# A hybrid decoder trunk on one core: branch gates by seven products, the residual stream in DRAM, h in whole rows

## The chip, the core and the metric

The kernel runs on one core of a Trainium2 chip. The core has a matrix engine (TensorE, PE in the profile; its weight loads are PEld), a vector engine (VectorE, DVE), a scalar engine (ScalarE, ACT), GpSimd (POOL), which here only issues accumulating DMAs, and SyncE (SP), which issues nearly all other DMAs. Each engine works through its own queue in order and waits on semaphores. Matmul results land in PSUM, where the kernel holds eight tiles (banks) of 128 x 512 floats; everything else on chip lives in SBUF. The metric is the device time of one execution in microseconds (us); the median of the runs is given, and one further execution was profiled.

## What is computed

Two decoder layers over one sequence of 512 positions with 1024 channels, float32. In each layer three sub-layers add to a residual stream x:

```python
h = rms_norm(x, gn[0])
x = x + 0.5 * rms_norm(swiglu(h, w_ffn1_gate[l], w_ffn1_up[l], w_ffn1_down[l]), gn[1])
h = rms_norm(x, gn[2])
proj = h @ w_in[l]
hq, hf, hi, hg, aq, ak, av, gate_a, gate_b = jnp.split(proj, IN_SPLITS, axis=-1)
y_hg = hgrn2_mixer(hq, hf, hi, hg, lb_all[l], hgrn_head_gain[l]) @ w_branch_hgrn[l]
y_at = swa_sink_attention(aq, ak, av, attn_sinks[l]) @ w_branch_attn[l]
mixed = jax.nn.sigmoid(gate_a) * y_hg + jax.nn.sigmoid(gate_b) * y_at
x = x + rms_norm(mixed @ w_out[l], gn[3])
h = rms_norm(x, gn[4])
x = x + 0.5 * rms_norm(swiglu(h, w_ffn2_gate[l], w_ffn2_up[l], w_ffn2_down[l]), gn[5])
```

`swiglu` is `(silu(h @ w_gate) * (h @ w_up)) @ w_down` with 2816 inner channels. The mixer's projection has 4864 columns: four groups of 512 for a gated linear recurrence with four heads, attention queries (512), keys and values (128 each), and two groups of 1024 that gate the two branches (gate_a, gate_b).

## The kernel before

**Matmuls.** Every float32 operand of a large matmul is split into a rounded part (hi) and the rest (lo), and a product is three matmuls: hi x hi, hi x lo, lo x hi (`mm3`; line 103 issues each of them, line 110 the transposes). Weights are the stationary operand, 128 x 128 blocks; the moving operand is a row of h, 128 channels by 512 positions, or half of it (256). Only in `down` is it the other way round.

**Weights.** `Stream` brings them in units of 128 x 1024, eight blocks each. A unit is loaded by SyncE into one of four raw buffers (lines 184 and 187), and `split` makes hi on ScalarE (line 219) and lo. An item of kind u gets its lo from a subtraction on VectorE (line 226); kinds v, a and d get it from a negated copy on ScalarE (line 223) and an accumulating DMA from GpSimd (line 224). Items are split up to three ahead of the one in use (`AHEAD`), with six in flight at most.

**A pair of output blocks** (gate and up of an FFN, 128 columns each) can be computed in three ways. `project` runs through the eight blocks of one output with 512 positions a time. `twice` does the same in two halves of 256 positions. `fast` takes the pair as a 2 x 2 block matrix product (rows: the two outputs; columns: the two halves of the positions; the sum over 1024 channels in two halves of 512) and computes it by seven products of four blocks each instead of eight. For this it needs sums of weight quarters (items b and c: lines 206, 207, 212 and 213 on VectorE, in tiles `tt`), sums of the quarters of h (`sums()`, one call for two of the eight rows of h: line 496 adds hi and lo again, lines 344 to 347 make the combinations, lines 294 and 295 split them), and a recombination of the seven results on VectorE (lines 682, 684, 689, 690) and ScalarE (line 670).

**An FFN.** `quad` does the first two pairs. Then two pairs run by `twice` (`PLAIN` = 4 plain pairs; the very first FFN has `FIRST` = 6, in part by `project`), and the other 18 by `fast`. `gated` (lines 706, 707) applies the SiLU gate. `down` multiplies by the down weights with eight outputs at a time in all eight PSUM banks. Its last `TAIL` = 2 groups are done one block of 128 positions after the other: `post` scales the block (line 566) and adds it to the residual stream x (line 570), which stays in SBUF as `x_all` (16 KB in each partition), `norm` normalises it for the next sub-layer (lines 509 to 513, 576), and `turn` transposes it on TensorE and writes h as hi and lo. `Pre` holds h as whole rows (the mixer), `Halves` in one tile per row and half of the positions (the FFNs).

**The mixer.** `quad` projects heads 0 and 1 of the recurrence, then follow keys, queries and values, two token-wise projections, heads 2 and 3, and 16 branch steps: `branch` projects one block of 128 gate columns by `project`, takes tanh (line 1020), multiplies the branch output by four more blocks and joins both (line 1025). First the eight of the attention branch, then the eight of the recurrence branch. The recurrences of the heads and the attention blocks are generators that issue their small matmuls in between.

**Order.** TensorE's instructions keep the order in which the program writes them. That order is set by `Order`: a running estimate of TensorE's time, and for each generator a delay (`WAIT`) after which its next step is issued between two matmuls. The other engines' instructions are put in order by a planner when the kernel is built: program order is the priority, but ready work may go ahead of work that waits. Working tiles of 2 KB in a partition come from one pool (`big()`, 53 buffers, `SLOTS`); PSUM's eight banks are five `acc` and three `aux`.

## Time and profile before

| | us |
|---|---|
| median of the runs | 2177.47 |
| lowest run | 2176.96 |
| profiled execution | 2179.35 |
| its span in the profile | 2177.6 |
| TensorE busy (matmuls) | 2161.6 |
| VectorE busy | 1369.7 |
| ScalarE busy | 1043.5 |
| GpSimd busy | 124.2 |

The execution moves 262.55 MB by DMA, 121 GB/s on average. Times in the profile's views are microseconds from the start of the span unless marked ns. "Busy" for TensorE includes modelled pipeline ends, so two neighbouring matmuls overlap in it, and 99% busy does not say at what rate it works. A line number is a line of the kernel; a helper's line (103, 110, 219, 226) stands for everything that calls it, and the tile names behind it tell which.

### The profile page before, as it was taken

The page shows a single profiled execution, that of the slowest core. Times are in us where ns is not written, and L with a number is a line of the kernel's source. Part 1 is how long each engine was busy: PE and PEld are TensorE (multiplying, and loading weights), DVE is VectorE, ACT ScalarE, POOL GpSimd, SP SyncE. Part 2 cuts the span into 40 slices and gives each one's busy share as a digit, 9 for nine tenths or more (in the row PEclk, how much of TensorE's full clock was granted, in tenths as well). Part 3 has the DMA queues.
Part 4 walks back from the last instruction along what each step waited for, and adds up shares of the span by engine and source line. Part 5 has one row for each costly group of instructions (what it writes and reads, how often), then busy time and mean ns, then how long its engine had stood idle before and what let it go on. Part 6 is the DMA issues. An engine that isn't in the chain of part 4 may idle for free.

```text
span 2177.6 us, 34576 instructions
## 1 busy us (share of the span) xinstructions
PE 2161.6 (99%) x13625; PEld 1951.4 (90%) x13625; DVE 1369.7 (63%) x2381; ACT 1043.5 (48%) x1703; POOL 124.2 (6%) x148
## 2 busy tenths in 40 slices
PE   9999999999999999999999999999999999999998
PEld 7999988888888999998899998898788889999987
DVE  6887725856734768783487786267566438687823
ACT  6565515354423555562355554254543336565612
POOL 0111000000000011100001110000000000111000
PEclk9999999999999999999999999999999999999999
DMA  7587632211223258773237874322112332578721
GB/s 236 121 185 180 173 97 78 87 59 59 70 95 97 81 130 182 180 203 97 73 107 162 192 184 147 96 86 68 53 64 78 97 97 88 137 179 184 187 89 39
DMA packets 126131, 262.55 MB, mean 121 GB/s; under 512 B 13360, under 2 KB 71184, under 8 KB 125968
## 3 DMA queue, kind: packets, MB, share of 16 engines
q1 hardware_dynamic: 105088, 203.13, 29.7%
q0 software_dynamic: 20736, 57.16, 15.0%
q8 instruction: 107, 1.75, 0.3%
q14 instruction: 56, 0.46, 0.1%
q10 hardware_dynamic: 144, 0.05, 0.0%
HBM read 200.99 MB, written 2.15 MB: 93 GB/s over the span
## 4 chain that ended last, share of the span: by engine, by line
PE 95%; DVE 2%; DMA 1%; ACT 1%; issue 1%; SPq 0%; POOL 0%; DVEq 0%; POOLq 0%; ACTq 0%
PE acc L103 70%; PE aux L103 23%; PE aux L110 1%; DMA w<-wall 1%; PE acc L110 1%; DMA s<-xin 0%; DVE s L453 0%; DMA wlo<-w 0%; DVE s L940 0%; DVE wlo L226 0%; DVE s L771 0%; DMA g_sb<-gains 0%; DVE s L566 0%; ACT s L509 0%; DVE s L576 0%
## 5 line engine op out<-in xcount | busy, mean ns | idle before, releaser
L103 PE MATMUL acc<-s,whi 128*128 128x256 f32 (+1 forms) x5104 | 1096.1, 312 | 1.6 <-ACT whi L219 0.9
L103 PEld LDWEIGHTS acc<-s,whi 128*128 128x128 f32 x5104 | 833.2, 191 | 48.3 <-DVE s L701 1.1
L103 PE MATMUL acc<-s,wlo 128*128 128x256 f32 (+1 forms) x2552 | 791.0, 310 | 0.1
L219 ACT CAST whi<-w 128x1024 fp32r<-128x1024 f32 (+1 forms) x373 | 360.7, 969 | 664.0 <-PE aux L103 270.0
L226 DVE TENSOR_TENSOR wlo<-w,whi 128x1024 fp32r<-128x1024 f32 (+1 forms) x229 | 278.5, 1218 | 405.1 <-ACT whi L219 399.6
L103 PEld LDWEIGHTS acc<-s,wlo 128*128 128x128 f32 x2552 | 487.2, 191 | 26.2 <-DVE wlo L226 0.4
L103 PE MATMUL acc<-whi,s 128*128 128x512 f32 x1296 | 425.2, 393 | 0.0
L103 PEld LDWEIGHTS acc<-whi,s 128*128 128x128 f32 x1296 | 243.9, 188 | 51.3
L103 PE MATMUL acc<-wlo,s 128*128 128x512 f32 x648 | 252.9, 390 | 0.0
L224 POOL DMA_DIRECT2D wlo<-w x144 | 124.0, 861 | 1909.9 <-DVE s L347 689.0
L103 PE MATMUL aux<-whi,s 128*128 128x512 f32 x624 | 207.8, 390 | 0.0
L103 PE MATMUL aux<-s,whi 128*128 128x256 f32 x1120 | 204.6, 283 | 0.0
L226 DVE TENSOR_TENSOR wlo<-tt,whi 128x1024 fp32r<-128x1024 f32 x140 | 170.6, 1218 | 10.1 <-ACT whi L219 9.7
L103 PEld LDWEIGHTS aux<-s,whi 128*128 128x128 f32 x1120 | 174.7, 192 | 0.0
L219 ACT CAST whi<-tt 128x1024 fp32r<-128x1024 f32 x140 | 145.7, 1041 | 26.8 <-PE acc L103 26.3
L103 PE MATMUL aux<-s,wlo 128*128 128x256 f32 x560 | 158.5, 283 | 0.0
L103 PEld LDWEIGHTS acc<-wlo,s 128*128 128x128 f32 x648 | 122.1, 188 | 23.7
L103 PEld LDWEIGHTS aux<-whi,s 128*128 128x128 f32 x624 | 117.1, 188 | 24.1
L206 DVE TENSOR_TENSOR tt<-w,w 128x512 f32<-128x512 f32 x70 | 48.4, 691 | 126.8 <-DMA w<-wall 116.9
L223 ACT ACTIVATE wlo<-w 128x1024 fp32r<-128x1024 f32 (+1 forms) x144 | 122.0, 847 | 0.0
L103 PE MATMUL aux<-wlo,s 128*128 128x512 f32 x312 | 121.4, 389 | 0.0
L103 PEld LDWEIGHTS aux<-s,wlo 128*128 128x128 f32 x560 | 107.5, 192 | 0.0
(164 smaller groups left out, 1888.2 us busy)
## 6 DMA issues: line engine op xcount, KB each, us to landing
w<-wall SPq DMA_DIRECT2D x283, 512.0 KB, 3.5
w<-wall SPq DMA_DIRECT2D x352, 128.0 KB, 2.6
wlo<-w POOLq DMA_DIRECT2D x74, 512.0 KB, 6.0
wlo<-w POOLq DMA_DIRECT2D x70, 256.0 KB, 4.1
grow<-rows_d SPq DMA_DIRECT2D x6, 512.0 KB, 4.9
s<-xin SPq DMA_DIRECT2D x8, 256.0 KB, 6.7
y<-s SPq DMA_DIRECT2D x8, 256.0 KB, 2.5
w<-wall SPq DMA_DIRECT2D x2, 256.0 KB, 4.1
```

The lines of the kernel that those rows point to most:

```text
L103: nc.tensor.matmul(o, lhsT, rhs, start=start, stop=stop)
L110: nc.tensor.transpose(o, src, ident)
L206: nc.vector.tensor_tensor(self.t13[:, h[0]], w[:, h[0]], v[:, h[0]], op=ALU.add)
L219: i = nc.scalar.copy(it.hi[:, c], w[:, c])
L223: nc.scalar.mul(it.lo[:, c], w[:, c], -1.0)
L224: nc.gpsimd.dma_start(it.lo[:, c].bitcast(F32), w[:, c], accum_op=ALU.add)
L226: nc.vector.tensor_tensor(it.lo[:, c], w[:, c], it.hi[:, c].bitcast(F32), op=ALU.subtract)
```

## The change

- **Branch gates.** The 16 gate blocks of a mixer are taken in eight pairs by the seven products. The body of `fast` up to the recombination becomes `sevenths`, and `branches` uses it. Its results for the second block come out negated, which the sign of tanh's scale takes back. Since the weights lie in DRAM as before, `gates` builds two of the three units of a pair from two half-row loads each. Four `sums()` calls are made in the mixer, ahead of heads 2 and 3.
- **Residual stream.** `x_all` goes. x lives in a DRAM tile `x_d`; `down` loads its eight pieces (128 x 512) into working buffers one group ahead of its tail, and `post` stores each piece after the addition. The first layout of x goes to DRAM as well.
- **Working buffers.** `SLOTS` goes from 53 to 61, the room of `x_all`.
- **h.** `Halves`, `of_half` and `twice` go; all sub-layers hold h in whole rows, and `Pre` gets `sums` and `raw`. `sums` adds hi and lo in whole rows of 512.
- **FFN.** `PLAIN` is 3: after `quad`'s two pairs one pair is done by `project`, and 19 by `fast`. All four `sums()` calls now stand ahead of that one pair.

```diff
--- before.py
+++ after.py
@@ -27,14 +27,14 @@
-SLOTS = 53
+SLOTS = 61
...
-W32, WS, AHEAD, TAIL, PLAIN, FIRST, EARLY = 4, 6, 3, 2, 4, 6, 4
+W32, WS, AHEAD, TAIL, PLAIN, FIRST, EARLY = 4, 6, 3, 2, 3, 6, 4
 HEADS = (0, 4, 1, 5, 2, 6, 3, 7)
@@ -111,12 +111,11 @@
         order.t += 107.0
-    x_all = const([P, TT, D], "x_all")
-    xt = [[x_all[:, t, h * S : (h + 1) * S] for h in range(2)] for t in range(TT)]
     g_sb = const([P, DEPTH, 6, KT], "g_sb")
     nc.scalar.dma_start(g_sb, gains)
     xs = [big() for _ in range(KT)]
     nc.sync.dma_start(xs[0], xin[:, 0, :])
+    x_d = dr.tile([TT, 2, P, S], F32, name="x_d")
     rows_d = dr.tile([DEPTH * 6 * KT, P], F32, name="rows_d")
     ones = const([P, P], "ones")
     nc.vector.memset(ones, 1.0)
@@ -158,6 +157,15 @@
             for _ in range(n):
                 self.items += [Item("a", self.n), Item("b", self.n), Item("c", self.n), Item("d", self.n, 4)]
                 self.n += 2
+
+        def gates(self):
+
+            u, h = self.n, (slice(0, D // 2), slice(D // 2, D))
+            self.src[u + 1] = [(h[0], wall[u + 1][:, h[1]]), (h[1], wall[u + 2][:, h[0]])]
+            self.src[u + 2] = [(h[0], wall[u + 1][:, h[0]]), (h[1], wall[u + 2][:, h[1]])]
+            self.pairs(1)
+            self.plain(1)
         def rows(self, kt):
@@ -355,7 +363,7 @@
         def operand(self, n):
             if n in (1, 2, 4):
-                return [[v[:, i, :] for i in range(2)] for v in self.raw(n // 4, n > 1)]
+                return self.raw(n // 4, n > 1)
             x, i = (self.x56, n - 5) if n in (5, 6) else (self.x37, (n - 3) // 4)
             return [[v[:, i, :] for v in x[k]] for k in range(4)]
@@ -398,7 +406,9 @@
                     p = aux()
                     for k in range(4):
                         transpose(p[:, k * P : (k + 1) * P], xs[4 * h + k][:, t * P : (t + 1) * P])
-                    (nc.vector.tensor_copy if h else nc.scalar.copy)(xt[t][h], p)
+                    x = big()
+                    (nc.vector.tensor_copy if h else nc.scalar.copy)(x, p)
+                    nc.sync.dma_start(x_d[t, h], x)
                     yield WAIT["laid"]
             self.laid = True
@@ -419,9 +429,9 @@
                 x.append(v)
         def raw(self, half, i):
-            return [x[half + i] for x in self.x124]
-
-    class Pre:
+            return [[x[half + i][:, j, :] for j in range(2)] for x in self.x124]
+
+    class Pre(Quarters):
         def __init__(self, l, n):
@@ -430,6 +440,20 @@
             self.have = [0, 0]
             self.rb = None
             self.xn = {}
+            self.x56, self.x37 = [], []
+
+        def sums(self):
+            k = len(self.x56)
+            a = []
+            for hi, lo in (self.h[k], self.h[k + 4]):
+                f = big()
+                nc.vector.tensor_tensor(f, hi.bitcast(F32), lo.bitcast(F32), op=ALU.add)
+                a.append([f[:, c] for c in HALF])
+            for x, v in zip((self.x56, self.x37), quarter_sums(a[0][0], a[1][0], a[0][1], a[1][1])):
+                x.append(v)
+
+        def raw(self, half, i):
+            return [cut(self.h[k + 4 * i], HALF[half]) for k in range(4)]
         def turn(self, half, get):
@@ -456,50 +480,6 @@
                     )
                 self.have[half] += 2
-    class Halves(Pre, Quarters):
...
-        def sums(self):
-            k = len(self.x56)
-            f = [big(F32, [P, 2, S // 2]) for _ in range(2)]
-            for half in range(2):
-                for i in range(2):
-                    h = self.h[k + 4 * i][half].bitcast(F32)
-                    nc.vector.tensor_tensor(f[half][:, i, :], h[:, 0, :], h[:, 1, :], op=ALU.add)
-            for x, v in zip((self.x56, self.x37), quarter_sums(f[0][:, 0, :], f[0][:, 1, :], f[1][:, 0, :], f[1][:, 1, :])):
-                x.append(v)
-
-        def raw(self, half, i):
-            return [self.h[k + 4 * i][half] for k in range(4)]
-
     def rms(parts, n, between=lambda h: None):
         ss = small([P, 2], "ss2", 8)
@@ -521,7 +501,7 @@
         nc.sync.dma_start(grow, rows_d[(l * 6 + n) * KT : (l * 6 + n + 1) * KT, :].rearrange("k p -> (k p)").partition_broadcast(P))
         y = [[acc(), acc()], [acc(), acc()], [acc(), aux()], [aux(), aux()]]
-        pre = (Pre if nxt[1] == 2 else Halves)(*nxt) if nxt else None
+        pre = Pre(*nxt) if nxt else None
         def ready(n):
@@ -534,7 +514,13 @@
             mv = [w.rearrange("p (m two c) -> p m two c", two=2, c=P)[:, :, i, :] for w in b[2:]]
             mm3(y[t][h], st, mv, 2 * j + i == 0, 2 * j + i == kt - 1)
+        xt = [[None] * 2 for _ in range(TT)]
         for j in range(kt // 2 - TAIL):
+            if j == kt // 2 - TAIL - 1:
+                for t in range(TT):
+                    for h in range(2):
+                        xt[t][h] = big()
+                        nc.sync.dma_start(xt[t][h], x_d[t, h])
             for h in range(2):
                 ready(2 * j + 2 + EARLY)
                 b = ws.next(8, TT)
@@ -568,6 +554,8 @@
             rc = rms(y[t], D, scale)
             for h in range(2):
                 nc.vector.scalar_tensor_tensor(xt[t][h], yg[h], rc, xt[t][h], op0=ALU.mult, op1=ALU.add)
+                if pre:
+                    nc.sync.dma_start(x_d[t, h], xt[t][h])
         def norm(t):
             rc = rms(xt[t], D)
@@ -602,12 +590,6 @@
             order.until(lambda: left[0] == 0)
         return pre
-    def of_half(pre, k, half):
...
     def quad(pre, halves):
         o = [acc() for _ in range(4)]
@@ -620,17 +602,8 @@
                 for j in range(4):
                     if (k, j) not in blocks:
                         blocks[k, j] = ws.next(uses=2 if halves else 1)
-                    wmm(o[j][:, c], blocks[k, j], of_half(pre, k, half), k == 0, k == KT - 1)
+                    wmm(o[j][:, c], blocks[k, j], cut(pre.h[k], c), k == 0, k == KT - 1)
             ws.pinned = False
-        return o
-
-    def twice(pre):
-
-        o = acc()
-        blocks = [ws.next(uses=2) for _ in range(KT)]
-        for half in (0, 1):
-            for k in range(KT):
-                wmm(o[:, HALF[half]], blocks[k], of_half(pre, k, half), k == 0, k == KT - 1)
         return o
     def project(pre):
@@ -650,44 +623,52 @@
                 order.poll()
         return o
+    H2 = S // 2
+
+    def sevenths(pre, between=lambda: None):
+
+
+        def product(o, it, c, n):
+            x = pre.operand(n)
+            for k in range(4):
+                wmm(o, ws.block(it, c + k), x[k], k == 0, k == 3)
+
+        p1, p26, p57, p43 = acc()[:, :H2], acc(), acc(), aux()
+        s, v = big()[:, :H2], big(F32, [P, 2, H2])
+        m = sb.tile([P, 4, H2], F32, tag="m", name=nm("m"), bufs=1)
+        w = ws.whole()
+        product(p1, w, 0, 1)
+        nc.scalar.copy(s, p1)
+        product(p26[:, :H2], w, 4, 2)
+        between()
+        w = ws.whole()
+        product(p57[:, :H2], w, 0, 5)
+        product(p57[:, H2:], w, 4, 7)
+        c = ws.whole()
+        product(p26[:, H2:], c, 0, 6)
+        pairs = [p.rearrange("p (i t) -> p i t", i=2) for p in (p26, p57, p43)]
+
+        nc.vector.tensor_tensor(m[:, 0:4:2, :], pairs[0], s.unsqueeze(1).to_broadcast([P, 2, H2]), op=ALU.add)
+
+        nc.vector.tensor_tensor(v, pairs[1], m[:, 2:3, :].to_broadcast([P, 2, H2]), op=ALU.add)
+        w = ws.whole()
+        product(p43[:, H2:], w, 4, 3)
+        product(p43[:, :H2], c, 4, 4)
+
+        nc.vector.tensor_tensor(m[:, 3, :], p57[:, :H2], v[:, 1, :], op=ALU.add)
+        nc.vector.tensor_tensor(m[:, 1:3, :], pairs[2], v[:, ::-1, :], op=ALU.add)
+        return m
+
     def fast(pre, a, start):
-
-
-        def product(o, it, c, n):
-            for k in range(4):
-                wmm(o, ws.block(it, c + k), X[n][k], k == 0, k == 3)
-
-        X = {n: pre.operand(n) for n in range(1, 8)}
...
+        def early():
             if j == FT - 1:
                 for i in range(EARLY):
                     a[i] = split(a[i])
-            w = ws.whole()
-            product(p57[:, :H2], w, 0, 5)
-            product(p57[:, H2:], w, 4, 7)
-            c = ws.whole()
-            product(p26[:, H2:], c, 0, 6)
-            pairs = [p.rearrange("p (i t) -> p i t", i=2) for p in (p26, p57, p43)]
-
-            nc.vector.tensor_tensor(m[:, 0:4:2, :], pairs[0], s.unsqueeze(1).to_broadcast([P, 2, H2]), op=ALU.add)
-
-            nc.vector.tensor_tensor(v, pairs[1], m[:, 2:3, :].to_broadcast([P, 2, H2]), op=ALU.add)
-            w = ws.whole()
-            product(p43[:, H2:], w, 4, 3)
-            product(p43[:, :H2], c, 4, 4)
-
-            nc.vector.tensor_tensor(m[:, 3, :], p57[:, :H2], v[:, 1, :], op=ALU.add)
-            nc.vector.tensor_tensor(m[:, 1:3, :], pairs[2], v[:, ::-1, :], op=ALU.add)
+
+        for j in range(start, FT):
+            m = sevenths(pre, early)
+            z = big(F32, [P, 2, H2])
             nc.scalar.activation(out=m[:, 0:2, :], in_=m[:, 0:2, :], func=AF.Silu)
             nc.vector.scalar_tensor_tensor(z, m[:, 0:2, :], -1.0, m[:, 2:4, :], op0=ALU.mult, op1=ALU.mult)
             a.append(z.rearrange("p i t -> p (i t)"))
@@ -727,9 +708,9 @@
             fast(pre, a, FIRST)
         else:
             for j in range(2, PLAIN):
-                if j < 4:
-                    pre.sums()
-                gated(twice(pre), twice(pre))
+                pre.sums()
+                pre.sums()
+                gated(project(pre), project(pre))
             fast(pre, a, PLAIN)
         return down(a, FT, l, n + 1, nxt)
@@ -1010,20 +991,25 @@
             gv = g.rearrange("p (i d) -> p i d", i=H)
             nc.vector.tensor_tensor(gv, gv, hgh[:, l : l + 1, :].to_broadcast([P, H, P]), op=ALU.mult)
             gs.append(g)
+        for _ in range(4):
+            pre.sums()
         for i in range(2, H):
             head(i, project(pre), project(pre))
-        def branch(m, get):
-            p = project(pre)
-            g = big()
-            nc.scalar.activation(out=g, in_=p, func=AF.Tanh, scale=0.5)
-            p = acc()
+        def branches(get):
+
+            v = sevenths(pre)
             src = get()
-            for k in range(4):
-                wmm(p, ws.next(), src[k], k == 0, k == 3)
-            nc.vector.scalar_tensor_tensor(g, g, 1.0, p, op0=ALU.add, op1=ALU.mult)
-            return g
+            for i in range(2):
+                g = big(F32, [P, 2, H2])
+                nc.scalar.activation(out=g, in_=v[:, 2 * i : 2 * i + 2, :], func=AF.Tanh, scale=-0.5 if i else 0.5)
+                p = acc()
+                for k in range(4):
+                    wmm(p, ws.next(), src[k], k == 0, k == 3)
+                g = g.rearrange("p i t -> p (i t)")
+                nc.vector.scalar_tensor_tensor(g, g, 1.0, p, op0=ALU.add, op1=ALU.mult)
+                yield g
         def attended():
             order.until(lambda: left[0] == 0)
@@ -1033,24 +1019,26 @@
             order.until(lambda: None not in oa)
             return oa
-        part = [branch(m, attended) for m in range(KT)]
+        part = [g for m in range(0, KT, 2) for g in branches(attended)]
         mixed = []
-        for m in range(KT):
-            g = branch(m, recurred)
-            nc.vector.tensor_tensor(g, g, part[m], op=ALU.add)
-            mixed.append(split(g, 0.5))
+        for m in range(0, KT, 2):
+            for g in branches(recurred):
+                nc.vector.tensor_tensor(g, g, part[len(mixed)], op=ALU.add)
+                mixed.append(split(g, 0.5))
         return down(mixed, KT, l, 3, nxt)
     for l in range(DEPTH):
         for n in (0, 2, 4):
             if n == 2:
-                ws.plain((4 * H + 4 + 2 + 2 * KT) * KT // 8 + 2 * KT * 4 // 8)
+                ws.plain(2 * H + 6 + 8)
+                for _ in range(KT):
+                    ws.gates()
                 ws.rows(KT)
             else:
                 p = FIRST if l + n == 0 else PLAIN
-                ws.plain(8)
-                ws.plain(2 * p - 8, "v")
+                ws.plain(min(2 * p, 8))
+                ws.plain(max(2 * p - 8, 0), "v")
                 ws.pairs(FT - p)
                 ws.rows(FT)
     pre = First()
```

39 lines of the change are left out of this document (removed).

## The prediction

> **What bounds the kernel now.** I read the page first, then the chain of work in order of time, then busy time by windows, then groups of instructions. The page:
>
> ```profile
> span 2177.6 us, 34576 instructions
> PE 2161.6 (99%) x13625; PEld 1951.4 (90%) x13625; DVE 1369.7 (63%) x2381; ACT 1043.5 (48%) x1703; POOL 124.2 (6%) x148
> PEclk9999999999999999999999999999999999999999
> PE 95%; DVE 2%; DMA 1%; ACT 1%; issue 1%; SPq 0%; POOL 0%; DVEq 0%; POOLq 0%; ACTq 0%
> ```
>
> TensorE carries 95% of the chain at full clock; only a shorter list of matmuls, or a new wait in front of one, moves the end. A busy PE says nothing of its rate, so the rates come from long pieces of the chain (start us, length us, what):
>
> ```profile
> 597.51 99.99 PE acc L103 x441
> ...
> 747.77 46.08 PE acc L103 x384
> ...
> 806.80 7.20 PE acc L103 x60
> 816.88 7.20 PE acc L103 x60
> ```
>
> The first piece is branch work in layer 0, all 512 columns wide: 99.99 / 441 = 0.2267 us each. The second is the quad and the `twice` pairs of an FFN, all 256 wide: 46.08 / 384 = 0.1200 us. Twice the columns cost 1.89 times, so half-width matmuls carry some 0.013 us of their own each. The last two lines are the same place in neighbouring pairs of `fast`: 10.08 us apart = 84 x 0.1200, with no gap.
>
> **The matmuls removed.** A pair of 128-column outputs over 1024 inputs takes three matmuls per block. Seven products: 7 x 4 x 3 = 84 at 256 = 10.08 us. By `project`: 2 x 8 x 3 = 48 at 512 = 10.88. By `twice`: 96 at 256 = 11.52.
> - Gates: 8 pairs a layer go from 10.88 to 10.08: 0.80 x 16 = 12.8 us.
> - FFNs two to four: two `twice` pairs (23.04) become one `project` pair and one fast pair (20.96): 2.08 x 3 = 6.2 us. The first FFN keeps its six plain pairs.
>
> Together 19.1 us, all on the chain. The Trainium skill, TensorE: Matmul & The Clock Gate, section Back-to-back issue gap, gives a gap of N/2.4 + 2.5 ns; the trace has 13 ns where it has 2.5, and by its figures the same sum would be 23.3 us (an estimate); I go by the rows.
>
> **What is added on VectorE.** Groups by shape (mean ns after the comma), then the busy time of the engines by windows:
>
> ```profile
> L226 DVE TENSOR_TENSOR wlo<-tt,whi 128x1024 fp32r<-128x1024 f32 x140 | 170.6, 1218 | 10.1 <-ACT whi L219 9.7
> L295 DVE TENSOR_TENSOR s<-s,s 128x512 fp32r<-128x512 f32 x120 | 76.6, 684 | 2.1 <-ACT s L294 1.9
> L206 DVE TENSOR_TENSOR tt<-w,w 128x512 f32<-128x512 f32 x70 | 48.4, 691 | 126.8 <-DMA w<-wall 116.9 <-issue 9.7
> L684 DVE TENSOR_TENSOR s<-acc,m 128x512 f32<-128x512 f32 x70 | 48.4, 692 | 2.4
> L682 DVE TENSOR_TENSOR m<-acc,s 128x512 f32<-128x512 f32 x70 | 47.9, 684 | 5.6 <-PE acc L103 5.6
> L690 DVE TENSOR_TENSOR m<-aux,s 128x512 f32<-128x512 f32 x70 | 47.7, 681 | 4.4 <-PE aux L103 4.4
> L689 DVE TENSOR_TENSOR m<-acc,s 128x256 f32<-128x256 f32 x70 | 29.7, 424 | 2.2
> L496 DVE TENSOR_TENSOR s<-s 128x256 f32<-128x256 f32 x48 | 17.0, 416 | 0.0
> ```
> ```profile
> core 0: us, PE busy (x) PEld busy (x) DVE busy (x) ACT busy (x) POOL busy (x), PEclk, DMA share, GB/s
> 500.00:510.00 10.00, 10.00 (x60) 8.53 (x60) 1.83 (x4) 5.63 (x12) 0.00 (x0) 1.00 0.29 97
> 510.00:540.00 30.00, 29.94 (x175) 25.16 (x175) 21.04 (x46) 14.99 (x30) 0.00 (x0) 1.00 0.16 53
> 540.00:570.00 30.00, 29.82 (x153) 25.68 (x152) 27.46 (x84) 9.62 (x17) 0.00 (x0) 1.00 0.26 82
> 570.00:600.00 30.00, 29.95 (x165) 25.66 (x164) 16.05 (x38) 13.78 (x18) 0.00 (x0) 1.00 0.24 76
> 600.00:690.00 90.00, 90.00 (x399) 74.53 (x398) 37.39 (x42) 28.27 (x35) 0.00 (x0) 1.00 0.30 95
> 807.00:957.00 150.00, 150.00 (x1252) 150.00 (x1251) 115.67 (x161) 87.99 (x120) 25.81 (x30) 1.00 0.81 185
> 1610.00:1650.00 40.00, 39.82 (x203) 34.21 (x202) 35.25 (x96) 14.59 (x26) 0.00 (x0) 1.00 0.25 80
> ```
>
> A gate pair: items b and c add four half-row adds (4 x 0.69 = 2.76 us); the three low-part subtractions stay three; the recombination adds 0.684 + 0.692 + 0.424 + 0.681 = 2.48. That is 5.2 us more per pair. A `sums()` call is two adds at 512 (0.68 each), four at 256 (0.42 each) and two low parts (0.68 each): 4.4 us, so four are 17.7 us more in each mixer.
>
> From 600 on this is free: VectorE is busy 37.4 of 90 us there and would be at about 67 (30 us for some 5.8 pairs); `fast` itself, 807 to 957, runs without a gap at 115.7 of 150. ScalarE (28.3 of 90) takes about 3.7 us more a pair (two negated copies, casts for five items instead of three, one PSUM copy), still far from full. GpSimd's two accumulating DMAs a pair are asked for some 12 us ahead and come every 10.08 us in `fast`. I cost all three at nothing.
>
> From 500 to 600 it is not free. Heads 2 and 3 run their recurrences beside the first branches, and TensorE follows an order written at build time. VectorE's idle time: 8.2 us in 500:510, 9.0 in 510:540, 2.5 in 540:570, 13.9 in 570:600. The chain passes through VectorE in that stretch already:
>
> ```profile
> 566.74 0.42 DVE s L785
> 567.16 0.20 DVE s L771
> ...
> 569.07 0.21 DVE s L834
> 569.28 0.14 issue
> 569.42 1.10 PE aux L103 x4
> ```
>
> So a microsecond of lateness there is about one on the end. Bookkeeping: if the four sums fill the gap from 502 on (h has long been there), 17.1 of 17.7 us are absorbed by 540; then pair one (5.2) and the adds of pair two (2.8) meet 2.5 us of idle, and VectorE is 0.6 + 8.0 - 2.5 = 6.1 us behind at 570; 570:600 clears it. If the sums start only behind the gated values (their program position, about 518), some 7.7 us are absorbed by 540, and it is 10.0 + 5.5 = 15.5 behind at 570. Bounds per layer: 0 (weight items are asked for three ahead and can yield to the recurrences) to 15.5. I take 4, two thirds of the 6.1, since the adds are not in the recurrences' path. Layer 1 is as dense (35.25 of 40). Two layers: +8.
>
> **FFN start.** VectorE by timeline, second FFN:
>
> ```profile
> 775.91 1.42 DVE L496 TENSOR_TENSOR s<-s 128x256 f32<-128x256 f32 x4
> ...
> 779.14 1.29 DVE L295 TENSOR_TENSOR s<-s,s 128x512 fp32r<-128x512 f32 x2 [0.23 <-ACT s L294]
> 786.75 0.69 DVE L707 TENSOR_TENSOR s<-acc,s 128x512 f32<-128x512 f32 x1 [6.31 <-PE acc L103]
> ```
>
> The last sum ends at 780.4; `fast` starts at 786.7, its product 5 (the first to need sums) 24 matmuls later at 789.5: 9.1 us to spare. In the changed kernel `fast` starts 12.2 us earlier (10.88 instead of 23.04 after the quad): product 5 at 777.4. VectorE is rid of 4 x 0.3 us (four adds of 0.416 become two of 0.684) and of up to two subtractions (2.4): its sums end between 776.8 and 779.2. The wait is 0 to 1.9 us; I take 0.7: +2 over three FFNs.
>
> **x in DRAM, whole rows.** SyncE's queue and VectorE at a boundary, and two DMA groups:
>
> ```profile
> 735.63 0.33 SPq L187 DMA_DIRECT2D w<-wall  x1
> ```
> ```profile
> 733.05 1.42 DVE L570 SCALAR_TENSOR_TENSOR x_all<-s,rt,x_all 128x512 f32<-128x512 f32 x2
> ```
> ```profile
> y<-s SPq DMA_DIRECT2D x8, 256.0 KB, 2.5
> s<-xin SPq DMA_DIRECT2D x8, 256.0 KB, 6.7
> ```
>
> Each store waits on SyncE for its L570, and weight loads queue behind it. The load issued at 735.63 comes just after the L570 of block 2 ends (734.5), so a store ahead of it costs an issue slot of 0.33 us, or up to 1.4 if L570 slips; that load fills a buffer for a unit wanted after the quad, over 20 us later. Each `down` loads eight 256 KB pieces over 10.9 us before the tail and 5.4 more before the first `post`; even at 6.7 us each, overlapped as those of xin are, they land in time. The eight stores of `lay` fall in the first FFN's start. I cost all at 0; without cover a weight load or an x piece would be late by 0 to 2 us in each of six sub-layers, 12 at most. Whole rows change neither the count nor the width of the copies that fill h. The product p43 holds one of three `aux` banks for 24 matmuls and a 0.68 us read; where recurrences want the same banks this is 0 to 0.7 us for some three pairs a layer; taken at 0.
>
> **Sum.** The profiled execution took 2179.35 us (span 2177.6). 2179.35 - 19.1 + 8 + 2 = 2170.3; the median of the runs, 2177.47, lies 1.9 lower, so the forecast is **2168.5 us**.
>
> **Rivals.**
> - *All hidden.* VectorE puts the sums in the gap at 500 and the recurrences ahead of everything. For it: 43 idle us of 100 there against some 36 added. Against: 27.46 of 30 in 540:570. 2177.47 - 19.1 = 2158.4.
> - *Slower: VectorE's lateness in the mixer outgrows the matmuls saved.* Place: heads 2 and 3; price 15.5 us a layer, and 1.9 an FFN: 2177.47 - 19.1 + 31 + 5.7 = 2195. It is slower than before from (19.1 - 2) / 2 = 8.5 us a layer on. For it: program order, and the tight chain above. Against: VectorE's planner runs ready work in gaps.
> - *Buffers run out.* Counted from the code, while heads 2 and 3 run, 46 of the 53 working buffers are alive (h 16, attention and head outputs 12, values and gates 8, the heads 9, a branch 1). The 16 of the sums make it 62, of 61. If head 3 had to wait for head 2, from its start here
>
> ```profile
> 539.96 0.54 DVE L863 TENSOR_SCALAR s<-s,oml,lb 128x512 f32<-128x512 f32 x1
> ```
>
>   to the end of the recurrences at 597.5, up to 40 us a layer would be lost: about 2238. One buffer short is more likely a delay of a copy.
> - *The clock.* Layer 1, where attention makes TensorE wait:
>
> ```profile
> 1550.00:1560.00 10.00, 8.94 (x56) 7.08 (x56) 6.87 (x17) 2.23 (x6) 0.00 (x0) 0.86 0.01 2
> 1560.00:1570.00 10.00, 9.67 (x69) 7.81 (x67) 4.04 (x11) 7.12 (x21) 0.00 (x0) 0.97 0.18 52
> ```
>
>   The granted clock lost 0.14 and 0.03 of 10 us: 1.7 us for one dip. If three new waits a layer brought a dip each, 6 x 1.7 = 10: 2179. The Trainium skill, TensorE: Matmul & The Clock Gate, section Part 1: The HAM clock gate, says that an idle window of about 3.4 us halves the clock; the dip here agrees in size, and the rule speaks against a change that adds waits.
>
> **Chances.** Forecast (2160 to 2176) 0.45; all hidden 0.17; lateness in the mixer (2176 to 2195) 0.25; clock 0.08; buffers 0.05. A range of 2157 to 2193 leaves out the buffer case, the top of the second rival and a little at the bottom, some 0.15. Two per cent, about what a measurement of this kernel can tell from no change, is 43.5 us: below 2134 would need more than twice the matmuls saved (0.01); above 2221 needs the buffer case or a mixture of the others (0.06); 0.93 lies between.
>
> **What would show it.** In the profile after: 16 gate pairs of 84 matmuls at 0.120 us; FFN pairs 10.08 us apart from one pair earlier; L496 gone, its successor 12 times in FFNs at two adds each and 8 times in mixers. Right on the mixer: waits of TensorE on VectorE of 2 to 6 us between 540 and 600, none from 610 on. Wrong, if TensorE waits on weights (wlo) in the later branches, on a DMA of x at a boundary, or if the granted clock dips in both mixers.

## Result and the profile after

The changed kernel takes **2228.66 us** (median, 2227.43 to 2230.39) where the kernel before takes 2177.22 in the runs beside it: a ratio of **1.0237, 95% interval 1.0217 to 1.0257**, slower by about 51 us. One of the four runs of the kernel before took 7588.77 us, the others 2176.92 to 2177.47, and the ratio goes by those others. The forecast was 2168.5. The profiled execution has a span of 2228.6 us.

The page of the kernel after (span; busy time by engine; TensorE's busy tenths and granted clock in 40 slices; the chain by engine):

```profile
span 2228.6 us, 36095 instructions
PE 2157.4 (97%) x14021; PEld 1969.5 (88%) x14021; DVE 1481.7 (66%) x2573; ACT 1107.6 (50%) x1810; POOL 156.9 (7%) x186
...
PE   8999999997899999999999999999978999999998
...
PEclk9999999998999999999999999999989999999999
...
PE 89%; DVE 7%; DMA 2%; ACT 1%; issue 1%; SPq 0%; POOL 0%; DVEq 0%; ACTq 0%; POOLq 0%
```

TensorE's share of the chain fell from 95% to 89%, and VectorE's rose from 2% to 7%. The loss sits in few places: slices 0, 9 and 10, 29 and 30 (counted from 0). The first root of each sub-layer's norm (an ACTIVATE on ScalarE, `rt<-ss`) is a landmark that both kernels have; the timeline of that tile by window, third sub-layer, kernel before and kernel after (durations, then first and last start):

```profile
L512 ACT ACTIVATE rt<-ss,rt x8: 294/295/326, 721.4 to 744.8; 128x1 f32<-128x1 f32 x8
```
```profile
L492 ACT ACTIVATE rt<-ss,rt x8: 294/295/296, 746.1 to 772.8; 128x1 f32<-128x1 f32 x8
```

Read so in each window, us from one first root to the next:

| stretch | before | after | difference | as forecast |
|---|---|---|---|---|
| start and first FFN | 346.3 | 352.0 | +5.7 | 0 |
| mixer, layer 0 | 375.1 | 394.1 | +19.0 | -2.4 |
| second FFN | 350.8 | 353.6 | +2.8 | -1.4 |
| third FFN | 350.9 | 354.7 | +3.8 | -1.4 |
| mixer, layer 1 | 376.7 | 394.2 | +17.5 | -2.4 |
| fourth FFN | 350.9 | 353.5 | +2.6 | -1.4 |
| end | 26.9 | 26.5 | -0.4 | 0 |

The differences add to 51.0, which is the spans' difference. (An FFN's stretch ends at the next norm, so a late FFN start counts in the stretch that it begins. The stretch of layer 1 before, 376.7, holds the dip of the clock that the prediction shows, 1.7 us; with the same gates it took 375.1 to 376.8 in other kernels below.)

**Mixer.** TensorE's waits over the whole span, kernel after (us in total, times, longest):

```profile
PE aux L110 <- DVE s L303: 27.7, 2, 13.8
PE aux L103 <- DVE s L752: 10.0, 8, 3.1
PE acc L110 <- DVE s L564: 9.3, 3, 3.2
PE aux L110 <- ACT s L951: 4.4, 2, 2.2
```

The first row is one wait of 13.8 us in each layer. VectorE's timeline there, layer 0 (start, duration, line and tiles; the brackets give the idle time before and what ended it):

```profile
515.44 1.23 DVE L234 TENSOR_TENSOR wlo<-tt,whi 128x1024 fp32r<-128x1024 f32 x1 [8.30 <-ACT whi L227]
...
522.08 1.29 DVE L992 TENSOR_TENSOR s<-s,hgh 128x512 f32<-128x512 f32 x2
523.28 1.29 DVE L450 TENSOR_TENSOR s<-s,s 128x512 f32<-128x512 f32 x2
...
528.05 1.28 DVE L450 TENSOR_TENSOR s<-s,s 128x512 f32<-128x512 f32 x2
...
531.20 0.28 DVE L303 TENSOR_TENSOR s<-aux,s 128x128 fp32r<-128x128 f32 x1
...
532.60 1.29 DVE L450 TENSOR_TENSOR s<-s,s 128x512 f32<-128x512 f32 x2
533.80 0.29 DVE L303 TENSOR_TENSOR s<-aux,s 128x128 fp32r<-128x128 f32 x1
...
535.00 0.29 DVE L303 TENSOR_TENSOR s<-aux,s 128x128 fp32r<-128x128 f32 x1
...
536.44 0.28 DVE L303 TENSOR_TENSOR s<-aux,s 128x128 fp32r<-128x128 f32 x1
...
537.24 1.29 DVE L450 TENSOR_TENSOR s<-s,s 128x512 f32<-128x512 f32 x2
```

The four sums (each begins with an L450 row) run as one block from 523.3 to 541.6, at their place in the program, behind the gated values (L992); the 8.30 us for which VectorE waited ahead of L234 held none of them. Four short splits that read attention's results out of an `aux` bank (L303 `s<-aux`) stand between them and end at 536.7. TensorE meanwhile needs an `aux` bank: its next instruction, a transpose, starts at 536.78. In the kernel before, by the same view, the corresponding splits (there L295) begin within 3 us of the gated values (L1011), and TensorE is idle for 0.3 us in all from 500 to 600:

```profile
516.41 1.28 DVE L1011 TENSOR_TENSOR s<-s,hgh 128x512 f32<-128x512 f32 x2
517.62 1.70 DVE L892 TENSOR_TENSOR s<-s,s 128x128 f32<-128x128 f32 x8
519.23 1.00 DVE L295 TENSOR_TENSOR s<-aux,s 128x128 fp32r<-128x128 f32 x2
```

Busy time of the engines by windows, kernel after (PE, PEld, DVE, ACT and POOL busy, then the granted clock):

```profile
520.00:530.00 10.00, 2.94 (x15) 2.08 (x13) 10.00 (x24) 1.16 (x2) 0.00 (x0) 0.79 0.00 0
530.00:540.00 10.00, 2.40 (x7) 1.58 (x7) 9.72 (x25) 3.25 (x8) 0.00 (x0) 0.50 0.00 0
540.00:550.00 10.00, 8.64 (x48) 7.88 (x49) 2.79 (x5) 5.93 (x10) 0.00 (x0) 0.69 0.00 1
...
570.00:580.00 10.00, 9.71 (x78) 9.54 (x77) 10.00 (x25) 6.35 (x11) 1.72 (x2) 1.00 0.77 186
580.00:590.00 10.00, 7.38 (x45) 6.19 (x44) 9.73 (x25) 3.67 (x7) 0.00 (x0) 1.00 0.28 65
590.00:600.00 10.00, 7.02 (x38) 6.01 (x39) 9.86 (x33) 4.44 (x7) 0.86 (x1) 1.00 0.60 172
...
770.00:780.00 10.00, 6.85 (x46) 6.62 (x45) 9.52 (x20) 6.49 (x15) 0.00 (x0) 0.83 0.45 152
```

Layer 0 can be added up. First hole: 7.06 + 7.60 + 1.36 = 16.0 us of idle. Clock: 2.40 us of work at 0.50 and 8.64 at 0.69 are worth some 1.2 + 2.7 = 3.9 us less (an estimate from the windows' mean clock). Second hole (570 to 600), where VectorE is full: 5.9 us; the chain runs there through L752 (recurrences), L220 and L221 (adds of the weights) and L234. Together 25.8; with 6.4 us of matmuls saved that is +19.4, against +19.0 measured. Layer 1 has the same three pieces (16.1, 3.8 and 6.0 us by its windows from 1620 to 1710).

**FFN starts.** The last window above lies in the start of the second FFN: 3.2 us idle, and a clock of 0.83. VectorE's timeline there, kernel after:

```profile
765.13 0.16 DVE L493 RECIPROCAL rt<-rt 128x1 f32<-128x1 f32 x1 [0.42 <-ACT rt L492]
766.65 0.69 DVE L214 TENSOR_TENSOR tt<-w,w 128x512 f32<-128x512 f32 x1 [1.36 <-DMA w<-wall]
767.26 0.88 DVE L564 TENSOR_SCALAR s<-s,rt 128x512 f32<-128x512 f32 x2
768.05 0.68 DVE L215 TENSOR_TENSOR tt<-w 128x512 f32<-128x512 f32 x1
```

L214 and L215 are the first two adds of the weights of the FFN's first fast pair. L214 waits 1.36 us for a weight load, and the norm (L564), whose operand is ready at 765.3, waits behind it. Of two plain pairs the kernel after has left one, so these adds come two weight units earlier than before, among the norms. In the kernel before, at the same place, the norm (there L576) follows its reciprocal at once:

```profile
740.20 0.15 DVE L513 RECIPROCAL rt<-rt 128x1 f32<-128x1 f32 x1
740.39 0.88 DVE L576 TENSOR_SCALAR s<-x_all,rt 128x512 f32<-128x512 f32 x2
```

**Start.** The same at the very beginning: VectorE's timeline and one window, kernel after:

```profile
43.02 0.69 DVE L214 TENSOR_TENSOR tt<-w,w 128x512 f32<-128x512 f32 x1 [3.78 <-DMA w<-wall]
43.63 1.29 DVE L685 TENSOR_TENSOR s<-s,s 128x512 f32<-128x512 f32 x2
```
```profile
36.00:60.00 24.00, 19.24 (x89) 15.63 (x88) 19.07 (x46) 15.07 (x22) 1.72 (x2) 0.86 0.74 211
```

Before, the same stretch, by the same views (L704 is the gating, after L685; L206 is the first add, after L214):

```profile
39.76 1.28 DVE L704 TENSOR_TENSOR s<-s,s 128x512 f32<-128x512 f32 x2
...
42.30 0.69 DVE L206 TENSOR_TENSOR tt<-w,w 128x512 f32<-128x512 f32 x1 [0.98 <-DMA w<-wall]
```
```profile
36.00:60.00 24.00, 22.40 (x114) 18.27 (x113) 21.90 (x52) 18.27 (x29) 2.58 (x3) 1.00 0.66 160
```

Before, the gating ran ahead of the add; after, it stands behind it. TensorE has 3.2 us more idle, and 0.14 of 19.2 us (2.7, an estimate) lost to the clock: 5.9, against 5.7 measured.

**What went as costed.** The later branches, in the chain of the kernel after:

```profile
634.99 12.66 PE acc L103 x84
650.53 12.66 PE acc L103 x84
```

They are 15.54 us apart, as 84 matmuls at 0.1200 for the gates and 24 at 0.2267 for the branches' products make 15.52. (The 84 of one row are 60 of the gates and the 24 products; the other 24 of the gates go to an `aux` bank in the 2.88 us between two rows.) And x, in the page's DMA issues (KB each, us to landing):

```profile
x_d<-s SPq DMA_DIRECT2D x48, 256.0 KB, 2.0
s<-x_d SPq DMA_DIRECT2D x48, 256.0 KB, 4.5
```

### The profile page after: what moved, and what is told of

It reads as the page before. It is cut to its first block, busy times and chain, and to the rows that moved or that the text cites. A ratio compares the mean times of both kernels' runs of the same rounds, so it can differ in the third digit from the quotient of the medians.

```text
span 2228.6 us, 36095 instructions
## 1 busy us (share of the span) xinstructions
PE 2157.4 (97%) x14021; PEld 1969.5 (88%) x14021; DVE 1481.7 (66%) x2573; ACT 1107.6 (50%) x1810; POOL 156.9 (7%) x186
## 4 chain that ended last, share of the span: by engine, by line
PE 89%; DVE 7%; DMA 2%; ACT 1%; issue 1%; SPq 0%; POOL 0%; DVEq 0%; ACTq 0%; POOLq 0%
PE acc L103 63%; PE aux L103 24%; PE aux L110 2%; DMA w<-wall 1%; DVE wlo L234 1%; DVE s L752 1%; DVE s L477 1%; DVE s L303 0%; DVE s L450 0%; DMA s<-xin 0%; DMA wlo<-w 0%; ACT s L489 0%; PE acc L110 0%; DVE s L552 0%; DVE s L564 0%
## 5 line engine op out<-in xcount | busy, mean ns | idle before, releaser
L103 PE MATMUL acc<-s,whi 128*128 128x256 f32 (+1 forms) x5064 | 1042.7, 304 | 0.7 <-DVE s L682 0.7
L227 ACT CAST whi<-w 128x512 fp32r<-128x512 f32 (+1 forms) x373 | 352.0, 945 | 561.5 <-PE aux L103 300.4
L234 DVE TENSOR_TENSOR wlo<-w,whi 128x1024 fp32r<-128x1024 f32 (+1 forms) x191 | 231.9, 1217 | 324.5 <-ACT whi L227 311.0
L232 POOL DMA_DIRECT2D wlo<-w x182 | 156.7, 861 | 1928.6 <-ACT wlo L231 1682.2
L103 PE MATMUL aux<-s,whi 128*128 128x256 f32 x1424 | 261.3, 284 | 0.0
L234 DVE TENSOR_TENSOR wlo<-tt,whi 128x1024 fp32r<-128x1024 f32 x178 | 217.0, 1219 | 50.2 <-ACT whi L227 50.2
L103 PEld LDWEIGHTS aux<-s,whi 128*128 128x128 f32 x1424 | 222.4, 192 | 0.1
L227 ACT CAST whi<-tt 128x1024 fp32r<-128x1024 f32 x178 | 185.5, 1042 | 46.4 <-PE acc L103 44.7
L103 PE MATMUL aux<-s,wlo 128*128 128x256 f32 x712 | 201.5, 283 | 0.0
L214 DVE TENSOR_TENSOR tt<-w,w 128x512 f32<-128x512 f32 x89 | 61.6, 692 | 151.4 <-DMA w<-wall 138.8
L231 ACT ACTIVATE wlo<-w 128x1024 fp32r<-128x1024 f32 (+1 forms) x182 | 154.0, 846 | 0.2
```

The source lines that it names most:

```text
L103: nc.tensor.matmul(o, lhsT, rhs, start=start, stop=stop)
L214: nc.vector.tensor_tensor(self.t13[:, h[0]], w[:, h[0]], v[:, h[0]], op=ALU.add)
L227: i = nc.scalar.copy(it.hi[:, c], w[:, c])
L231: nc.scalar.mul(it.lo[:, c], w[:, c], -1.0)
L232: nc.gpsimd.dma_start(it.lo[:, c].bitcast(F32), w[:, c], accum_op=ALU.add)
L234: nc.vector.tensor_tensor(it.lo[:, c], w[:, c], it.hi[:, c].bitcast(F32), op=ALU.subtract)
```

## Experiments

Stretches below are read by the first roots, as in the table. Without any wait added, a mixer would take 375.1 - 6.4 = 368.7 us and an FFN 350.9 - 2.08 = 348.8.

**The FFN part alone, in the kernel before.**

The rows of h are whole, x stays in `x_all`, and the gates are as before (code in part):

```diff
-W32, WS, AHEAD, TAIL, PLAIN, FIRST, EARLY = 4, 6, 3, 2, 4, 6, 4
+W32, WS, AHEAD, TAIL, PLAIN, FIRST, EARLY = 4, 6, 3, 2, 3, 6, 4
...
-                gated(twice(pre), twice(pre))
+                pre.sums()
+                pre.sums()
+                gated(project(pre), project(pre))
```

> The kernel before with only the FFN part: h in whole rows, one plain pair by project, 19 fast pairs; x stays in SBUF, gates as before. Theory A (VectorE's queue: the weight sums of the first fast pair now stand ahead of the norms at an FFN's start and wait there for a weight DMA): three FFN starts lose about 4.2 us each and the FFNs gain 3.7 us in all, so about 2186 us. Rival B (the stores of x in SyncE's queue make that weight late): without the stores the starts lose nothing, so 2177 - 6 + 2 = about 2173 us.

2188.71 us, ratio 1.0043 (1.0027 to 1.0060): it is a loss by itself. FFNs two to four take 354.7, 353.4 and 353.5 us, the mixers 376.7 and 376.8. VectorE's timeline at the second FFN's start in this kernel:

```profile
743.42 0.69 DVE L215 TENSOR_TENSOR tt<-w,w 128x512 f32<-128x512 f32 x1 [1.25 <-DMA w<-wall]
744.03 0.88 DVE L555 TENSOR_SCALAR s<-x_all,rt 128x512 f32<-128x512 f32 x2
```

The same order as after, with x still on chip. So the late FFN start needs neither the DRAM stream nor the gates.

**x in DRAM alone, in the kernel before.**

```diff
-SLOTS = 53
+SLOTS = 61
...
+                    nc.sync.dma_start(x_d[t, h], x)
...
+                        xt[t][h] = big()
+                        nc.sync.dma_start(xt[t][h], x_d[t, h])
```

> The kernel before with only x in DRAM and 61 working buffers. Theory A: only the first 50 us change (the layout of x stands elsewhere in VectorE's queue), +5.7 us, so about 2183 us. Rival B (stores of x delay weights at FFN starts): +5.7 and three times 4.2, about 2196 us.

2181.88 us, ratio 1.0012 (1.0003 to 1.0022). The first root comes at 349.4 instead of 346.3; all later stretches are as before (375.1, 350.9, 350.9, 375.5, 350.9). At the boundaries x in DRAM costs nothing; at the start it costs 3.1 us, about half of what theory A said. There VectorE's adds of weights stand ahead of the first gating, as in the kernel after. That this order is the cause is read from the trace, and the last variant below shows that it can't be all of it. The eight added buffers come with the same edit, so the two are not told apart.

**The gates undone, in the kernel after.**

```diff
-        for _ in range(4):
-            pre.sums()
...
-        part = [g for m in range(0, KT, 2) for g in branches(attended)]
+        part = [branch(m, attended) for m in range(KT)]
```

> The changed kernel with its gates undone: 16 single blocks by project again, no sums in the mixer. If the three parts add up: 2177 + 5.7 (start) + 12.6 (three FFN starts) - 3.7 (FFNs) = about 2192 us, and both mixers take as long as before (344 us from the chain's first long piece to the tail of down).

2191.02 us, ratio 1.0053 (1.0038 to 1.0068). Mixers 375.2 and 376.8, as before the change; FFNs 355.1, 353.2, 353.5. The gates own 37.6 of the 51 us (37.2 by the spans of the profiled executions); the medians of the two runs above lie 9.2 and 2.4 us over that of the kernel before on their chip, so the three parts alone make 49 of it.

**No sums in the mixer, in the kernel after.** This kernel leaves the four mixer sums out; the products that need them read rows of h instead.

```diff
-        for _ in range(4):
-            pre.sums()
+        for k in range(4):
+            v = tuple(x.rearrange("p (i c) -> p i c", i=2) for x in pre.h[k])
+            pre.x56.append(v)
+            pre.x37.append(v)
```

> The changed kernel without the four sums in each mixer: products 3, 5, 6 and 7 of the gates read rows of h in place of the sums of its quarters, so the gates are not those of the reference. Theory A (the sums run as one block of some 20 us on VectorE and the reads of two aux banks by attention stand behind them, so TensorE stands still): each mixer gets 22 us shorter, about 2185 us. Rival C (the mixer's VectorE simply has too much to do between 500 and 600, and each microsecond of it counts once): 2 x 10 to 15 us, 2200 to 2209 us.

2191.79 us, ratio 1.0058 (1.0042 to 1.0074). Mixers 376.1 and 375.6 instead of 394.1 and 394.2: the sums cost 18.0 and 18.6 us a layer, about all of their 17.7 us on VectorE. It does not come down to the 2185 of the first theory, because 7 us a layer are left, and they sit in the second hole: in this kernel TensorE is idle for 5.9 us from 550 to 590, with a clock of 0.83 from 560 to 570.

**Neither sums nor adds.** As the last, and the second and third units of each gate pair take their weights as loaded, without the half-row adds.

```diff
-            if it.kind == "b":
+            if it.bare:
+                w = w if it.kind == "b" else v
+            elif it.kind == "b":
```

> e4 without the four half-row adds of each gate pair as well: items b and c of a gate pair take the weights as they are, and the products read rows of h in place of sums, so the gates are not the reference's. e4's mixers took 343 us, as long as before, where the matmuls are 6.4 us fewer. Theory A (the adds run between the recurrences' steps from 547 to 600): each mixer 4 to 6 us shorter, 2179 to 2184 us. Rival E (what is left in the mixer comes from the recombination or the aux bank it holds): no change, 2191 us.

2178.61 us, ratio 1.0001 (0.9991 to 1.0010). Mixers 369.7 and 369.6: the adds cost 6 us a layer, and what is left is within 1 us of the saving by matmuls alone. So everything else that the seven products add in the mixer (the accumulating DMAs, the PSUM bank of product p43, ScalarE's copies) costs 1 us a layer at most.

**The sums spread**, in the kernel after: from the second token projection on, one every 4 us.

```diff
+        def quarter():
+            for _ in range(4):
+                pre.sums()
+                yield 4000.0
+
+        order.spawn(quarter())
...
-        for _ in range(4):
-            pre.sums()
```

> The changed kernel with the four sums of a mixer issued by a generator, one every 4 us of TensorE's planned time from the second token projection on, instead of in one go behind it. Theory A (the block is what costs): VectorE has 10 to 13 us free between 500 and 518, the aux banks of attention are read between the sums, TensorE's stand of 24 us shrinks to 5 to 12: 2228 minus 2 x 12 to 19, 2190 to 2204 us. Rival C (the amount of VectorE work counts wherever it stands): no change, 2220 us or more.

2221.29 us, ratio 1.0195 (1.0180 to 1.0211), a miss for the theory that the block is what costs. Mixers 388.8 and 389.1: of the 37 us that the sums cost some 10 came back, 5 in each mixer (the median shows 7, since the FFNs take 3 us more here). VectorE's timeline and TensorE's waits from 480 to 620 in this kernel:

```profile
489.54 0.41 DVE L921 SCALAR_TENSOR_TENSOR s<-dist,aux 128x256 f32<-128x256 f32 x1
489.87 0.68 DVE L450 TENSOR_TENSOR s<-s,s 128x512 f32<-128x512 f32 x1
490.47 0.68 DVE L926 TENSOR_REDUCE mxs<-s 128x2 f32<-128x512 f32 x1
```
```profile
PE aux L110 <- DVE s L921: 4.6, 2, 4.3
PE aux L103 <- DVE s L752: 4.3, 3, 3.2
```

The sums now stand among attention's scores (L921) and row maxima (L926), and TensorE waits there. So it isn't the block alone: spread out beside attention and the recurrences, the sums still cost 13 us a layer of their 17.7.

**The first adds behind the norms**, on the kernel with the FFN part alone: the two adds of the first fast pair's second unit keep their place in the program.

```diff
+                if it.first:
+                    pin(i)
```

> e1 with one thing added: the two adds of item b of each FFN's first fast pair are held behind what the program has put on VectorE's queue before them (the norms of the last sub-layer among it). Theory A: the three FFN starts lose the 4.7 us again and the 6.2 us of matmuls come out, 2177 - 6 = about 2171 us. If the adds then come too late for the first fast pair, 2173 to 2180. Rival D (VectorE's amount of work at the start counts, not its order): as e1, 2188 us.

2177.73 us, ratio 0.9999 (0.9989 to 1.0008), where it was 1.0043 without. FFNs 350.6, 350.7 and 351.0. The order was the cause of the late starts (2.5 to 4.1 us an FFN came back), but 1.8 to 2.2 us an FFN of the saving stay lost. TensorE's timeline in the second FFN of this kernel, product 5 of the first fast pair:

```profile
778.45 0.38 PE L103 MATMUL acc<-s,whi 128*128 128x256 f32 x1 [0.52 <-ACT s L308]
779.18 0.39 PE L103 MATMUL acc<-s,whi 128*128 128x256 f32 x1 [0.34 <-DVE s L309]
```

It waits for the high and low parts of the sums: with one plain pair the sums come late. These waits are 0.9 us, TensorE's idle time in that FFN 1.0 us; the rest of the 1.8 isn't seen as a wait.

**Two plain pairs**, in whole rows, in the kernel before.

`PLAIN` stays 4 (code in part):

```diff
-                gated(twice(pre), twice(pre))
+                pre.sums()
+                gated(project(pre), project(pre))
```

> The kernel before with h in whole rows and two plain pairs by `project` per FFN (PLAIN 4; x stays in SBUF, gates as before, no pin). Each FFN two to four exchanges two pairs of 11.52 us for two of 10.88: 1.28 x 3 = 3.8 us fewer matmuls. Theory S (with one plain pair the sums end 2 us behind product 5 of the first fast pair, which is why the pinned variant's FFNs take 350.6 us against 350.9 of before in place of 348.8): here fast starts 10.88 us later, product 5 waits for nothing, FFNs take 349.6 us and the median is 2174 us (2172 to 2176). Theory W (whole rows themselves cost about 2 us an FFN, whatever the number of plain pairs): FFNs take 351 to 352 us, median 2177 to 2181. If the first fast pair's adds overtake the norms although they come one unit earlier only, 3 to 4 us are added at each of three FFN starts: 2184 or more.

2175.12 us, ratio 0.9985 (0.9976 to 0.9994). FFNs 349.8 each, 1.1 us below before (1.28 by matmuls), with no wait of TensorE at the second FFN's start. It lies inside theory S's range; whole rows themselves cost 0.2 us an FFN at most.

**Gates late**, in the kernel after: the attention branch's four pairs by `project`, the sums one by one beside the last of them, seven products for the recurrence branch's four pairs only, and the FFNs' pinned adds.

```diff
+LATE = 4
...
+        part = []
+        for m in range(0, KT, 2):
+            if m // 2 == LATE:
+                order.until(lambda: len(pre.x56) == 4)
+            for g in (plain if m // 2 < LATE else branches)(attended):
+                part.append(g)
+                if len(part) == 2 * LATE - 4:
+                    order.spawn(quarter())
```

> The changed kernel put in another order: the four pairs of the attention branch by project as before, the sums one by one beside the last of them, seven products only for the four pairs of the recurrence branch; the adds of each FFN's first fast pair held back as in e8. Theory A: mixers as before less 4 x 0.8 = 3.2 us each, FFNs less 6.2 us, the start of the kernel 3 to 5 us longer as in e2 or not, if the same hold cures it: 2177 - 6.4 - 6.2 + (0 to 5) = 2165 to 2170 us. Rival C: the sums and adds cost their 17.7 and 11 us a layer here too, 2200 us or more.

2173.82 us, ratio 0.9978 (0.9969 to 0.9988): above the expected 2165 to 2170, but 0.2% below the kernel before. Mixers 372.0 and 372.0, where 375.1 - 3.2 = 371.9 is all that four pairs can save. The same sums, the same adds a pair (for four pairs in place of eight), and nothing lost: it is the place. What is missing are the FFNs (350.6 to 350.7: the late sums again) and 1.4 us at the start.

**One pair earlier** (`LATE` = 3).

> The variant with late gates (seven products in the recurrence branch's four pairs alone, 2173.8 us), with the last pair of the attention branch by seven products as well; the sums come one pair earlier. Theory A (what costs is only that the sums and adds stand among attention's and the recurrences' steps, which end before this pair): one pair more of 10.08 us for 10.88 in each mixer, 2 x 0.80 less: 2172.2 us. Rival R (heads 2 and 3 still run beside that pair): the added 5.2 us of VectorE work or the sums come late by 3 us or more a layer: 2178 us or more, with waits of TensorE on VectorE's L752-like copies in 560 to 600.

2175.12 us, ratio 0.9985 (0.9976 to 0.9994), between the two numbers and on the rival's side of the variant before. Mixers 372.8 and 372.9: 0.8 more where 0.8 less was to come. One window of this kernel, and the same of the variant with `LATE` = 4:

```profile
580.00:600.00 20.00, 18.79 (x99) 15.45 (x99) 19.36 (x48) 11.75 (x18) 0.86 (x1) 1.00 0.22 54
```
```profile
580.00:600.00 20.00, 19.95 (x107) 16.74 (x106) 15.78 (x35) 12.17 (x16) 0.00 (x0) 1.00 0.16 54
```

VectorE has no room left there (19.36 of 20 us), TensorE is idle 1.2 us, and each mixer loses 1.7 us against what its fifth pair could bring. The start took 1.5 us more in the profiled execution than with `LATE` = 4: TensorE's waits there are the same, but the clock was 0.93 from 36 to 60, where it was 1.00. So the two medians do not compare the mixers alone; the stretches do.

**Both mended**: gates late (`LATE` = 4) with two plain pairs.

> The variant with late gates (2173.8 us; its FFNs take 350.7 us by the norms' first root) with two plain pairs by `project` per FFN in place of one, sums one a pair. Theory S: FFNs of 349.6 us, 3 x 1.1 = 3.3 us less: 2170.5 us (2169 to 2172). Theory W: FFNs of 351 to 352 us, 2174 to 2178 us.

**2169.85 us, ratio 0.9964 (0.9951 to 0.9976)**, the fastest, 0.4% below the kernel before. FFNs 349.8, 349.8 and 349.7, mixers 372.0 and 372.0, as theory S said. The start is still 3.2 us later than before. VectorE's first gating and the window in this kernel:

```profile
39.68 1.29 DVE L692 TENSOR_TENSOR s<-s,s 128x512 f32<-128x512 f32 x2 [0.40 <-ACT s L690]
```
```profile
36.00:60.00 24.00, 21.11 (x100) 17.13 (x99) 18.64 (x45) 17.19 (x25) 2.17 (x3) 0.93 0.79 226
```

The pinned adds no longer stand ahead of the first gating, and yet TensorE waits, now 1.5 us for a copy of x's layout by ScalarE and 0.5 for one by VectorE (L417), and the clock is 0.93. So with x in DRAM the start is late under either order on VectorE; with x on chip and the adds pinned, the first root came at 345.5, 0.8 us earlier than before. Whether the stores, the added buffers or the order on ScalarE do it, no run here tells.

## Why the prediction was wrong

**Matmuls removed: right.** Gates at 10.08 us a pair in the later branches, and mixers of 369.7 us once VectorE's additions are gone.

**What is added on VectorE: the step that failed, in its size.** The work (17.7 us of sums, 5.2 us a pair) and the place were right, even the second bookkeeping's guess that the sums keep their program position behind the gated values. The term was 4 us a layer and measured 24 to 25: 394.1 and 394.2 against the 369.7 and 369.6 without sums and adds. The fault is in "some 7.7 us are absorbed by 540": idle time of VectorE was set against the sums as if it did not matter what stands behind them. But VectorE ran them in one go, and the short reads that free attention's `aux` bank stood between them; each came later by the sums ahead of it, and TensorE waited 13.8 us for the last of the four. On balance nothing was absorbed: the price was the whole 18 us, some 4 of them given up by the clock, and 6 for the adds. The upper bound of 15.5 was too low for the same reason. The chain of before could not show this: from 505 to 550 it stays on TensorE, and the piece through VectorE that the prediction shows begins at 566.7. What TensorE needs next from VectorE has to be read from the order of VectorE's queue.

The Trainium skill, TensorE: Matmul & The Clock Gate, section Architectural detail, says that ScalarE's and VectorE's queues are strict first in, first out. The traces agree: L214 stands 3.78 us at the head of VectorE's queue, with L685 behind it, whose operands ScalarE had finished by 40.1.

The idle time itself was misread as well. "43 idle us of 100" in the first rival does not come out of the windows shown: VectorE is busy for 66.4 of the 100 us, so 33.6 are idle, less than the 36 to be added.

**The sum, with what was measured.** The matmuls bring the forecast -19.1. The mixers' work on VectorE takes some 49 us in place of 8, the three FFNs 15 in place of 2, and the start 5.7 in place of 0: together the 51 us.

**That weight items "can yield to the recurrences": wrong** in 570 to 600, where L220, L221 and L234 take turns with L752 on the chain; TensorE is idle for 5.9 us there.

**FFN start: wrong place, too small.** The prediction looked at when the sums end (0.7 us taken, 1.9 as a bound) and not at what else moves up. The sums cost 1.8 to 2.2, at the bound. But the first fast pair's adds moved up as well and overtook the norms while waiting for a load, 2.5 to 4.1 us an FFN. The FFN part was costed at 4.2 us of gain and is 9 us of loss.

**x in DRAM: right at the boundaries (0), wrong at the start.** It costs 3.1 us alone and 5.7 with the rest and the dip of the clock. The prediction looked at the stores, not at the order on VectorE; that order stands ahead of the wait in the trace, but with the adds held back 1.4 to 3.2 us stay, so the cause is open in part.

**Rivals.** The slower one named the place and the point from which it decides, 8.5 us a layer; its price of 15.5 was 9 too low, and with it its 2195. The clock rival happened as well, in both mixers and at the start, as a consequence of the waits. Of buffers running out nothing is seen: while TensorE stands still, VectorE is busy (10.00 and 9.72 of 10 us). Of the signs named, "no wait from 610 on" held; "waits of 2 to 6 us between 540 and 600" held for the adds only (longest 3.1); the large one was earlier and 13.8 us long. The sign against the forecast, a dip of the clock in both mixers, came.

## What to carry to other kernels

Before setting added work against an engine's idle time, look at what stands behind it in the engine's queue: if another engine waits for that, the added work delays it by its full length, however much idle time there is elsewhere. Place such work behind the last step that another engine waits for; here the same sums cost 18 us a layer ahead of such steps and nothing behind them. When units of a stream are removed, everything later in the stream is asked for earlier: look at what the next such instruction waits for, and what stands behind it in its queue.

## Of the hardware, not expected

A wait of 13.8 us cost more than its length: the granted clock was 0.50 from 530 to 540 and 0.69 from 540 to 550, although TensorE was at work again from 537 on, some 3.9 us more in layer 0 and 3.8 in layer 1. The Trainium skill, TensorE: Matmul & The Clock Gate, section Part 1: The HAM clock gate, has the clock halved after one idle window of some 3.4 us; the 0.50 here agrees.

Shorter waits sufficed as well. The 3.2 us wait of the second FFN's start (L564 in the waits above) went with a clock of 0.83 in its window, worth some 1.2 us of the 6.85 worked there. In the kernel before, the dip of layer 1 that the prediction shows (0.86 from 1550 to 1560) follows waits of 0.7 and 0.3 us. And the same waits do not always bring a dip: layer 0 of that kernel has them too (0.7 and 0.3 us, ending at 478.2 and 480.2), its clock is 1.00 from 470 to 500, and its stretch is 1.6 us shorter. So a difference of up to some 1.6 us between two such stretches can be a dip that one of them had.
